# Two token tiles of the value stage in one PSUM bank, in a hybrid decoder layer

## The chip, the core and the metric

The kernel runs on one core of a Trainium2 chip. The metric is the device time of one execution in microseconds (us). A core has several engines that run beside each other, each through its own queue in order: TensorE for matmuls (PE in the profile, with its weight loads as PEld), VectorE (DVE), ScalarE (ACT), GpSimd (POOL) and SyncE (SP), which here issues nearly all DMA transfers. Matmuls write into PSUM, which the kernel uses as eight banks of 512 fp32 numbers in each of 128 partitions; ACT and DVE read the results out of it.

## The reference

One inference step of a one-layer decoder for a prompt of 1024 tokens and 64 sample tokens (8 sequences of 8), width 1024. What matters here is the first projection and its two token-major parts, the attention values v (256 columns) and the gMLP values gmlp_v (768 columns):

```python
def layer(x, norm_mix, w_in, ...):
    h = rmsnorm(x, norm_mix)
    q, k, v, gu, gv, ga, gb = split_in(h @ w_in)
    ...
    o, nk, nv = attn_prompt(q, k, v, sinks)      # or attn_sample
    vn = layernorm(jax.nn.gelu(gv), ln_g, ln_b)
    s = spatial_gating(jax.nn.gelu(gu), vn, ws, bs)
    merged = jax.nn.sigmoid(ga) * (o @ w_pa) + jax.nn.sigmoid(gb) * (s @ w_pb)
    x = x + merged @ w_out
    f, nconv = conv_ffn(rmsnorm(x, norm_ffn), w_up, conv_w, conv_b, w_down, conv_prev)
    return x + f, nk, nv, nconv, vn
```

## The kernel before

The tokens are handled in two groups: group 0 has the 64 sample tokens and the first 512 prompt tokens, group 1 the last 512. All products are made from numbers split into a high and a low part, so that one fp32 product is three matmuls (high by high, high by low, low by high).

The change lies in the **value stage**, the first stage of the kernel, from about 4.9 to 107 us of the span. There the tokens are the stationary operand and 256 columns of weights (`w2h`, `w2l`) stream past them; the result of one token tile, 128 tokens by 256 columns, takes half a PSUM bank. The sample tokens are a tile of their own ("s"): its stationary operand holds the high parts in one half of the partitions and the low parts in the other (`both` in `mm_tok`), so that it takes 16 matmuls, and its two halves are added after the read-out. A prompt tile takes 24 (8 pieces of the contraction, three matmuls each, L554).

The stage goes over its weights in eight passes of 256 columns. The first pass, gmlp_v's first third for group 0, is written out by itself with five banks at once (`ps5`), since it runs while x is still being loaded; the change leaves it alone. The other seven are calls of `tokens` (L601), in this order on PE, and are called pass 1 to 7 below:

| pass | group | columns | token tiles in order |
|---|---|---|---|
| 1 | 0 | gmlp_v, second third | s, 0, 1, 2, 3 |
| 2 | 0 | v | s, 0, 1, 2, 3 |
| 3 | 0 | gmlp_v, last third | s, 0, 1, 2, 3 |
| 4 | 1 | v | 4, 5, 6, 7 |
| 5 to 7 | 1 | gmlp_v, last, first and second third | 4, 5, 6, 7 |

For each tile `tokens` takes a bank, makes the matmuls, and calls `out`, which reads the bank: `gv_out` by one activation on ACT (gelu, with the token's scale `rst`; L596), `v_out` by one on ACT too (L569). For the sample tile both first go through `whole`: ACT copies one half out (L561), DVE adds the other half from the bank (L562), and the activation then reads the sum in SBUF. `gv_out` ends with a store by SP (`gvd`, L599). Between the tiles stand jobs for the other engines: in passes 1 and 2 `x_job`, which loads 128 rows of group 1's x into one of four buffers (`stg`, L354), splits it (`hh` on ACT, L44; `hl` on DVE, L45) and sums its squares (L667, L668).

Banks come from a pool of eight: seven that go round under the name `st` (`bank()`), and one named `mx` for the sums of squares (`stats_tok`, L499) behind which the token scales are made (`rst`: a square root on ACT, L500, and a reciprocal on DVE, L501). The tile framework makes a matmul that starts in a bank wait until the last reader of that bank is done; it tracks a bank as one whole. Between the passes `stats_all` (L511) takes banks of the same pool, and the next stage (`Chain.product`, L315) does so too.

What each engine runs, and in which order, is fixed at the end of the program by a table (`ORDER`, applied by `issue_order`): it names positions in each engine's list, so that the order stays as long as the list does.

Of the kernel before, what the change touches and what calls it, by code (L numbers as in the profile page):

```python
# [34 lines left out]
def layer(tc, a):  # L35
# [11 lines left out]
    with ExitStack() as top:  # L47
# [333 lines left out]
        with ExitStack() as ph1:  # L381
# [109 lines left out]
            def bank():  # L491
                return psa.tile([P, 512], F32, name="st")
# [53 lines left out]
            def mm_tok(ps, g, lo, w, k):  # L546
                (ah, al, both), (wh, wl) = hs[g][k], w
                if g == lo == 0:
                    todo = [(both, wh), (both, wl)]
                else:  # L550
                    ah, al = ah[:, lo:lo + P], al[:, lo - NS * (g == 0):][:, 0:P]
                    todo = [(ah, wh), (ah, wl), (al, wh)]
                for i, (u, v) in enumerate(todo):
                    PE.matmul(ps, u, v[:, k, :], start=k + i == 0, stop=k == KD - 1 and i == len(todo) - 1)  # L554
# [46 lines left out]
            def tokens(g, key, out, jobs, between=None):  # L601
                if key in (("v", 1), ("gv", 1, 2)):
                    wide[key] = wide[key[0], 0, *key[2:]]
                else:
                    W.get()
                    W.get()
                for i, (_, lo) in enumerate(groups[g]["toks"]):
                    ps = bank()[:, :256]
                    for k in range(KD):
                        mm_tok(ps, g, lo, wide[key], k)  # L610
                    if between and i == 0:
                        between()
                    out(i, ps)
                    if jobs:
                        jobs.pop(0)()
# [54 lines left out]

            jobs = [x_job(k) for k in range(KD)]
            tokens(0, ("gv", 0, 1), lambda i, ps: gv_out(0, i, 1, ps), jobs, first_out)
            tokens(0, ("v", 0), lambda i, ps: v_out(0, i, ps), jobs)
            stats_all(0)
            tokens(0, ("gv", 0, 2), lambda i, ps: gv_out(0, i, 2, ps), jobs)
            hs0o.close()
            t0h, xr = right(th0, "T0h"), right(xro, "xr")
# [352 lines left out]
            def acc2():  # L1030
                return pmm.tile([P, 1024], F32, name="mm")
# [388 lines left out]
            for c in range(KD):  # L1420
                xt = x_next(0, c)
                w, ps = W.get(), acc2()
# [60 lines left out]
            for c in range(KD):  # L1483
                xt = x_next(1, c)
                w, ps = W.get(1 if c < 7 else 4), acc2()
# [214 lines left out]
        with ExitStack() as ph3:  # L1700
# [109 lines left out]
            bank = [psd.tile([P, 512], F32, name="dn") for _ in range(6)]  # L1810
# [272 lines left out]
```

## Time and profile before

| | |
|---|---|
| time, median of 3 runs | 1491.72 us (1490.73 to 1493.11) |
| the profiled execution | 1490.81 us |
| its span, first to last instruction | 1489.1 us |
| TensorE clock granted, mean | 0.999 |
| PE busy | 99% of the span |
| DVE busy | 79% |
| ACT busy | 58% |
| POOL busy | 19% |

The span is cut by the profile into times from its first instruction, and all times below are counted so. A row of a timeline gives start, length, engine, line, operation, what it writes and reads, and how many like it were put together. A matmul's length is its latency: in a stream they begin 0.11 us apart and last 0.28 us each, so a PE that is busy all the time is not shown at its peak by that. A bracket at the end of a row tells how long the engine was idle ahead of it and who ended that.

### The profile page before, as it was taken

The numbers are of one execution on the slowest core, as the hardware profiler recorded it, in microseconds if no ns is written. First come the engines' busy times: TensorE is split into PE (matmuls) and PEld (weight loads), VectorE is DVE, ScalarE is ACT, GpSimd is POOL, SyncE is SP. The second block draws the span as 40 slices with busy tenths as digits, with TensorE's granted clock in tenths as the row PEclk, the third lists the DMA queues.
The fourth block names the chain that finished last, engine by engine and source line by source line (L and its number), as shares of the span: only waits on it lengthen the run. The fifth ranks groups of instructions, "written<-read, shape, count | busy, mean of one in ns | idle before, by whom it ended". The sixth has DMA issues, their size and how long they took to land.

```text
span 1489.1 us, 30035 instructions
## 1 busy us (share of the span) xinstructions
PE 1480.2 (99%) x11476; PEld 1445.6 (97%) x11476; DVE 1181.0 (79%) x1890; ACT 856.9 (58%) x1794; POOL 286.6 (19%) x392
## 2 busy tenths in 40 slices
PE   9999999999999999999999999999999999999998
PEld 9999999999998999998989999999999999999997
DVE  7888877655576887989578898898898888685586
ACT  8657776564465775864444554654565556363463
POOL 3002000010030222310234222332242222000002
PEclk9999999999999999999999999999999999999999
DMA  8687546764679757458977433332332316983354
GB/s 258 228 290 248 168 167 217 239 227 161 230 261 300 221 165 247 140 185 310 336 272 271 131 123 118 125 124 96 117 134 96 110 59 234 330 300 104 112 163 155
DMA packets 133791, 289.29 MB, mean 194 GB/s; under 512 B 15760, under 2 KB 35984, under 8 KB 133648
## 3 DMA queue, kind: packets, MB, share of 16 engines
q1 hardware_dynamic: 133504, 287.37, 57.6%
q8 instruction: 90, 1.47, 0.4%
q14 instruction: 53, 0.43, 0.1%
q10 hardware_dynamic: 144, 0.01, 0.0%
HBM read 198.77 MB, written 90.52 MB: 194 GB/s over the span
## 4 chain that ended last, share of the span: by engine, by line
PE 93%; DMA 2%; DVE 2%; issue 1%; ACT 1%; SPq 0%; POOL 0%; POOLq 0%; DVEq 0%; ACTq 0%
PE st L315 52%; PE mm L240 17%; PE dn L1725 11%; PE st L554 6%; PE sc L1221 2%; PE po L1272 2%; PE pt L1248 1%; DMA traw<-td 1%; DMA wraw<-wt 1%; PE mx L849 1%; DVE tl L41 1%; DVE wl L41 0%; DMA x<-xt 0%; PE po L1175 0%; ACT th L40 0%
## 5 line engine op out<-in xcount | busy, mean ns | idle before, releaser
L315 PE MATMUL st<-t,wh 128*128 128x288 f32 x2128 | 427.6, 294 | 0.0
L315 PEld LDWEIGHTS st<-t,wh 128*128 128x128 f32 x2128 | 335.6, 188 | 0.2
L315 PE MATMUL st<-t,wl 128*128 128x288 f32 x1064 | 311.8, 293 | 0.0
L315 PE MATMUL st<-th,wh 128*128 128x256 f32 x1064 | 294.6, 277 | 0.0
L315 PE MATMUL st<-tl,wh 128*128 128x256 f32 x1064 | 294.2, 277 | 0.0
L315 PE MATMUL st<-th,wl 128*128 128x256 f32 x1064 | 293.9, 276 | 0.0
L315 PEld LDWEIGHTS st<-th,wh 128*128 128x128 f32 x1064 | 199.8, 188 | 0.2 <-ACT kn L296 0.2
L315 PEld LDWEIGHTS st<-t,wl 128*128 128x128 f32 x1064 | 199.7, 188 | 0.0
L315 PEld LDWEIGHTS st<-th,wl 128*128 128x128 f32 x1064 | 199.7, 188 | 0.0
L315 PEld LDWEIGHTS st<-tl,wh 128*128 128x128 f32 x1064 | 199.7, 188 | 0.0
L40 ACT CAST wh<-wraw 128x512 fp32r<-128x512 f32 (+2 forms) x188 | 129.2, 700 | 87.4 <-DMA wraw<-wt 28.0
L1725 PE MATMUL dn<-th,wh 128*128 128x288 f32 (+1 forms) x616 | 176.8, 287 | 0.1
L1725 PE MATMUL dn<-tl,wh 128*128 128x288 f32 (+1 forms) x616 | 176.2, 286 | 0.0
L1725 PE MATMUL dn<-th,wl 128*128 128x288 f32 (+1 forms) x616 | 175.3, 285 | 0.0
L41 DVE TENSOR_TENSOR wl<-wraw,wh 128x512 fp32r<-128x512 f32 (+2 forms) x188 | 148.6, 804 | 26.4 <-ACT wh L40 24.4
L40 ACT CAST wh<-ws 128x512 fp32r<-128x512 f32 x168 | 102.7, 621 | 87.0 <-PE st L315 53.2
L41 DVE TENSOR_TENSOR wl<-ws,wh 128x512 fp32r<-128x512 f32 x168 | 117.5, 709 | 42.5 <-ACT wh L40 41.8
L1725 PEld LDWEIGHTS dn<-th,wh 128*128 128x128 f32 x616 | 115.6, 188 | 0.5 <-DVE x L1735 0.4
L1725 PEld LDWEIGHTS dn<-th,wl 128*128 128x128 f32 x616 | 115.9, 188 | 0.1
L1725 PEld LDWEIGHTS dn<-tl,wh 128*128 128x128 f32 x616 | 115.6, 188 | 0.1
L41 DVE TENSOR_TENSOR tl<-traw,th 128x544 fp32r<-128x544 f32 (+1 forms) x85 | 61.1, 723 | 21.1 <-ACT th L40 20.9
L40 ACT CAST th<-traw 128x544 fp32r<-128x544 f32 (+1 forms) x85 | 54.5, 642 | 38.2 <-PE dn L1725 29.2
(292 smaller groups left out, 3187.2 us busy)
## 6 DMA issues: line engine op xcount, KB each, us to landing
wraw<-wt SPq DMA_DIRECT2D x137, 512.0 KB
traw<-td SPq DMA_DIRECT2D x77, 272.0 KB
td<-za SPq DMA_DIRECT2D x22, 544.0 KB
q<-qd SPq DMA_DIRECT2D x16, 512.0 KB
upd<-hl SPq DMA_DIRECT2D x14, 512.0 KB
td<-t SPq DMA_DIRECT2D x11, 544.0 KB
wpart<-wt SPq DMA_DIRECT2D x22, 256.0 KB
qd<-q SPq DMA_DIRECT2D x8, 576.0 KB
```

Of the source, the lines that this page charges most:

```text
L40: S.copy(hi, src)
L41: V.tensor_sub(lo, src, hi.bitcast(F32))
L240: PE.matmul(ps[:, lo:lo + c1 - c0], u[:, k, :], v[:, c0:c1], start=(k == 0 and i == 0), stop=(k == nk - 1 and i == 2))
L315: PE.matmul(ps, u[:, kk, :], v, start=first and kk + i == 0, stop=kk == 3 and i == 2, skip_group_check=True)
L554: PE.matmul(ps, u, v[:, k, :], start=k + i == 0, stop=k == KD - 1 and i == len(todo) - 1)
L849: PE.matmul(ps[:, P * i:P * i + P], vn[:, i], late["wst"][:, c, :], start=True, stop=True)
L1221: PE.matmul(ps[:, h, o0:256], q, kst[kv][:, e, k0:cur + P], start=e == 0, stop=e == 1)
L1248: PE.transpose(pt[:, h * P:h * P + P], s[:, h, 0:P], ident)
L1272: PE.matmul(po, v[:, kv, :], t, start=e == 0, stop=last)
L1725: PE.matmul(place(m, e), u[:, m, :], v[:, lo:hi], start=new and i + k == 0 and (e == 0 or m % 2 == 0), stop=i == NU - 1 and k == 2, skip_g ...
```

## The change

In `tokens` the first tile and the third now share one bank, the second and the fourth another, each with a half of 256 columns; the fifth, where there is one, has a bank to itself. A pass of group 0 takes three banks in place of five, one of group 1 two in place of four. No instruction comes or goes, and every engine keeps its order.

```diff
@@ def tokens(g, key, out, jobs, between=None) @@
                 else:
                     W.get()
                     W.get()
+                banks = []
                 for i, (_, lo) in enumerate(groups[g]["toks"]):
-                    ps = bank()[:, :256]
+                    if i in (0, 1, 4):
+                        banks.append(bank())
+                    ps = banks[(0, 1, 0, 1, 2)[i]][:, 256 * (i in (2, 3)):][:, :256]
                     for k in range(KD):
                         mm_tok(ps, g, lo, wide[key], k)
```

What it changes is the bank that a matmul writes, and with it what the matmul waits for. PE's rows at the end of pass 1's second tile and the start of its third, before (`st` with its number is the bank's allocation, `h0` and so on the tokens, `w2h` and `w2l` the weights):

```order
L554 MATMUL st_579<-w2l_471,h7_444 128x256
L554 MATMUL st_579<-w2h_470,h7_444 128x256
L554 MATMUL st_616<-w2h_470,h0_296 128x256 [waits Activation_49]
L554 MATMUL st_616<-w2l_471,h0_296 128x256
L554 MATMUL st_616<-w2h_470,h0_296 128x256
```

And of the change, at the same place:

```order
L554 MATMUL st_579<-w2l_471,h7_444 128x256
L554 MATMUL st_579<-w2h_470,h7_444 128x256
L554 MATMUL st_517<-w2h_470,h0_296 128x256 [waits DVE_49]
L554 MATMUL st_517<-w2l_471,h0_296 128x256
L554 MATMUL st_517<-w2h_470,h0_296 128x256
```

The third tile waited for an activation of the pass before, the reader of a bank seven allocations back. Now it goes into `st_517`, the bank of the pass's own first tile, the sample's, and waits for DVE's addition out of it.

The start of pass 2's fourth tile on PE, before:

```order
L554 MATMUL st_815<-w2l_510,h7_444 128x256
L554 MATMUL st_815<-w2h_509,h7_444 128x256
L554 MATMUL st_860<-w2h_509,h0_296 128x256 [waits Activation_49]
L554 MATMUL st_860<-w2l_510,h0_296 128x256
L554 MATMUL st_860<-w2h_509,h0_296 128x256
```

And of the change:

```order
L554 MATMUL st_735<-w2l_510,h7_444 128x256
L554 MATMUL st_735<-w2h_509,h7_444 128x256
L554 MATMUL st_774<-w2h_509,h0_296 128x256 [waits Activation_49]
L554 MATMUL st_774<-w2l_510,h0_296 128x256
L554 MATMUL st_774<-w2h_509,h0_296 128x256
```

Both wait for ACT, but the one before for the activation that read pass 1's second tile, the one of the change for the activation that reads pass 2's own second tile, `st_774`.

## The prediction

> **What bounds the kernel now.** I read the page first: the busy times, then the chain that ended last.
>
> ```profile
> span 1489.1 us, 30035 instructions
> ...
> PE 1480.2 (99%) x11476; PEld 1445.6 (97%) x11476; DVE 1181.0 (79%) x1890; ACT 856.9 (58%) x1794; POOL 286.6 (19%) x392
> ...
> PE 93%; DMA 2%; DVE 2%; issue 1%; ACT 1%; SPq 0%; POOL 0%; POOLq 0%; DVEq 0%; ACTq 0%
> ```
>
> PE is the path: 93% of the chain. An average can hide stages with another limit, so the view of busy times by stretch comes next, from the end of the load-bound start (20 us) to the last matmuls; the first two numbers of a row are its length and PE's busy time.
>
> ```profile
> 20.00:107.00 87.00, 87.00 (x760) 86.56 (x759) 77.14 (x141) 57.90 (x107) 0.01 (x1) 1.00 0.78 253
> 107.00:447.00 340.00, 340.00 (x2776) 339.81 (x2775) 239.28 (x394) 206.02 (x413) 44.00 (x57) 1.00 0.64 213
> 447.00:660.00 213.00, 212.96 (x1464) 196.25 (x1463) 175.65 (x336) 145.46 (x438) 52.75 (x94) 1.00 0.63 203
> 660.00:1100.00 440.00, 440.00 (x3247) 425.03 (x3246) 372.06 (x519) 229.50 (x421) 120.34 (x152) 1.00 0.52 184
> 1100.00:1480.00 380.00, 379.88 (x3099) 379.27 (x3097) 300.15 (x474) 200.41 (x388) 53.88 (x68) 1.00 0.50 165
> ```
>
> The first row is the stretch in which all seven passes of the change run, the others are everything behind it. PE idles 0.00 us in the first and 0.04 + 0.12 us in the rest. The view of waits, from 20 us on, has one row for PE:
>
> ```profile
> PE fs L1770 <- DVE rt L1762: 0.6, 1, 0.6
> ```
>
> That row, at the very end, waits for work that itself waits for PE. Two things follow. The seven banks never hold PE up now, so taking fewer of them can win nothing. And a microsecond that PE loses before 107 us finds no gap behind it in which to be made good: it goes into the time whole, less at most 0.16 us.
>
> **What the change removes and adds.** No instruction is added, removed or moved. What goes are PE's waits for a bank seven allocations old, which cost 0.0 us by the row above. What comes: the third tile's first matmul waits until the first tile has been read out of the bank, and the fourth's until the second has. Before, a read-out could be late by several tiles; now it has one tile, the one between. So for each pass I compare the time at which PE reached the third and fourth tile with the end of the read-out that it must now wait for. PE's rows for pass 1 (start, length; in a row of x2 the second matmul starts 0.11 later, and it is the first of a tile):
>
> ```profile
> 26.30 0.39 PE L554 MATMUL st<-w2h,h 128*128 128x256 f32 x2
> 29.02 0.39 PE L554 MATMUL st<-w2h,h 128*128 128x256 f32 x2
> 31.74 0.39 PE L554 MATMUL st<-w2h,h 128*128 128x256 f32 x2
> 41.71 0.39 PE L554 MATMUL st<-w2h,h 128*128 128x256 f32 x2
> ```
>
> Third, fourth and fifth tile of pass 1 begin at 26.41, 29.13 and 31.85: 2.72 us for a tile of 24 matmuls. The last row is the fourth tile of pass 2, at 41.82. The read-outs of pass 1, from the timelines of DVE and ACT:
>
> ```profile
> 27.56 0.75 DVE L562 TENSOR_TENSOR gs<-st,gs 64x256 f32<-64x256 f32 x2
> 31.00 0.47 ACT L596 ACTIVATE gv<-st,rst 128x256 f32<-128x256 f32 x1
> ```
>
> The sample tile is read by a copy on ACT and then by the addition L562 on DVE; the second of the two in the row is pass 1's and ends at 28.31. The second tile's activation ends at 31.47. They are late because both engines first finish the pass before (whose scale, a square root, comes late) and the next group's x.
>
> Two small prices of a wait come from the first microseconds, where PE does wait:
>
> ```profile
> 7.44 0.75 DVE L538 SCALAR_TENSOR_TENSOR h<-x,c_gains,h 128x512 fp32r<-128x512 f32 x1 [0.61 <-ACT h L536]
> 8.24 0.51 PE L554 MATMUL st<-w2h,h 128*128 128x256 f32 x2 [0.17 <-DVE h L538]
> 7.34 0.39 PE L554 MATMUL st<-w2h,h 128*128 128x256 f32 x2
> ```
>
> DVE ends at 8.19 and PE starts at 8.24: 0.05 us from release to start. And the two matmuls behind that wait take 0.51 us where two in the stream take 0.39: 0.12 us for starting again.
>
> **Pass 1.** Third tile: 28.31 + 0.05 = 28.36, a stop of 1.95 us. Fourth: PE could be there at 28.36 + 0.12 + 2.72 = 31.20 but the read-out allows 31.47 + 0.05 = 31.52, 2.39 behind its old 29.13. These two stops are not added: read-outs that ACT and DVE do at their own pace set the hour. Fifth tile: 31.52 + 0.12 + 2.72 = 34.36, so PE is 2.51 us late.
>
> **Pass 2** depends on how much of this lateness ACT takes over. What stands queued behind the stop is all of PE's stream; who waits for it is ACT, with the fifth tile's read-out, then SP with its store, then two loads of x behind that store, then ACT again:
>
> ```profile
> 36.41 0.46 ACT L596 ACTIVATE gv<-st,rst 128x256 f32<-128x256 f32 x1
> 36.90 0.32 SPq L599 DMA_DIRECT2D gvd<-gv  x1
> 37.31 0.88 SPq L354 DMA_DIRECT2D stg<-xt  x2
> 42.68 0.72 ACT L44 ACTIVATE hh<-stg,c_gains 128x512 fp32r<-128x512 f32 x1 [0.99 <-DMA stg<-xt]
> 43.95 0.47 ACT L569 ACTIVATE gv<-st,rst 128x256 f32<-128x256 f32 x1
> ```
>
> The fifth tile now ends at 34.36 + 2.72 + 0.17 (a matmul's length beyond its share of the stream, 0.28 - 0.11) = 37.25, so ACT reads it at 37.30 in place of 36.41: 0.89 late. The store and both loads go out 0.89 later, the last load lands 0.89 later, and pass 2's second tile is read out at 44.42 + 0.89 = 45.31. The fourth tile starts at 45.36 against 41.82: PE is now 3.54 late, 3.66 with the restart. The two ends of this term: the loads may land when they did (a busy queue, not the issue, setting the hour), then ACT's wait of 0.99 us swallows the 0.89 and PE is 44.42 + 0.05 - 41.82 + 0.12 = 2.77 late; or ACT falls behind as far as PE, 2.77 + 2.51 = 5.28. I take 3.66, since SP issues in order and the two loads stand right behind the store.
>
> **Passes 3 to 7.** The rows of DVE, ACT and PE, in that order:
>
> ```profile
> 55.05 0.41 DVE L562 TENSOR_TENSOR gs<-st,gs 64x256 f32<-64x256 f32 x1
> 57.42 0.84 ACT L596 ACTIVATE gv<-st,rst 128x256 f32<-128x256 f32 x2
> 53.15 0.39 PE L554 MATMUL st<-w2h,h 128*128 128x256 f32 x2
> 61.63 0.47 ACT L596 ACTIVATE gv<-st,rst 128x256 f32<-128x256 f32 x1 [2.25 <-PE st L554]
> 67.48 0.48 ACT L569 ACTIVATE gv<-st,rst 128x256 f32<-128x256 f32 x1
> 67.86 0.28 PE L554 MATMUL st<-w2h,hh 128*128 128x256 f32 x1
> 79.14 0.47 ACT L596 ACTIVATE gv<-st,rst 128x256 f32<-128x256 f32 x1
> 79.87 0.28 PE L554 MATMUL st<-w2h,hh 128*128 128x256 f32 x1
> ```
>
> Pass 3: the third tile began at 53.26, now 56.92; the addition ended at 55.46, with ACT's 0.89 at 56.35: no stop. The fourth, at 55.98 + 3.66 = 59.64, has its read-out by 57.89 + 0.89. At 61.63 ACT has waited 2.25 us for PE: from here both engines shift by PE's 3.66, and only the old distances count. Pass 4: the read-out ended at 67.96, the third tile began at 67.86, so 68.01 - 67.86 = 0.15 of stop, and 0.12. Pass 5: read out at 79.61, 0.26 before the tile's 79.87; passes 6 and 7 come with more to spare. No stop there.
>
> **The sum** is 3.66 + 0.15 + 0.12 = 3.9 us. The profiled execution took 1490.81 us (span 1489.1), so it would be 1494.7; the median of the three runs shown, 1491.72, lies 0.91 above that execution, and the forecast stands on the median: **1495.6 us**.
>
> **Rivals.** *Nothing is lost: a later PE wait makes the time good, or the new wait does not bind* (not slower, 1491.7). Its place is behind 107 us, and it needs a PE wait of 3.9 us on something that does not wait for PE, such as a weight load. The stretches above show 0.16. For the second half: a wait is listed by engine, but its count in the built program is that of the second L562 addition for pass 1's third tile. Chance 0.09.
>
> *The x loads land when they did*: 2.77 + 0.27 = 3.0 us, 1494.8 on the median. For it: ACT's row at 42.68 waits for a load, and the DMA share is 0.78. Against: both loads stand behind the store on SP. Chance 0.12.
>
> *ACT falls behind as far as PE in pass 2*: 5.28 + 0.27 = 5.6 us, 1497.3. Against it: ACT reached the fifth tile at 36.41, 1.7 us after PE had done with it (31.85 + 2.72 + 0.17). Chance 0.06.
>
> *The clock drops in a stop.* At the start PE ran slower:
>
> ```profile
> 1.10:4.40 3.30, 3.25 (x15) 3.25 (x16) 0.81 (x3) 2.04 (x3) 0.76 (x2) 1.00 0.72 193
> 4.59 0.39 PE L620 MATMUL st<-c_ones 128*128 128x128 f32 x2
> ```
>
> 15 matmuls in 3.30 us are 0.22 each, and a little later the same pair is 0.11 apart (0.39 - 0.28). If a stop put PE back into that pace for another 3.3 us, half of it, 1.6 us, is lost: 1497.3. Against it: the short waits between 5 and 10 us did not slow PE, and the stop is one of 1.95 us. Chance 0.06. [...]
>
> **How the numbers follow.** Forecast 0.64, the four rivals 0.09, 0.12, 0.06 and 0.06, and 0.03 for a gain that I see no cause for. The range goes from the lowest run shown plus the low end (1490.73 + 3.04 = 1493.8, taken down to 1493.4 as the runs shown differ by 2.4 us) to 1497.6, which takes in the two dear rivals; nothing lost lies outside. A measurement of this kernel can tell about 0.2%, 2.98 us, from no change. The forecast passes that by 0.9 us, so of its 0.64 some 0.08 counts as the same; of the low rival two thirds. Slower 0.56 + 0.04 + 0.12 = 0.72, same 0.08 + 0.08 + 0.09 = 0.25, faster 0.03.
>
> **What would show it.** PE waits for DVE L562 once, about 1.95 us near 26.4; for ACT L596, about 0.3 near 31; for ACT L569, about 1.0 near 44 (PE there at 41.82 + 2.51 = 44.33, released at 45.36), and 0.15 near 71; no others. The busy row of the first stretch would lose PE busy time by these stops, 3.45 us, less the 0.17 us tail of the matmul before each, some 2.8 us, and every later stage would keep its old length. A stop of PE in passes 3, 5, 6 or 7, or a later stage of another length, would prove me wrong.

## The result, and the profile after

| | before | with the change |
|---|---|---|
| median | 1491.61 us (16 runs, 1490.42 to 1494.23) | 1495.60 us (16 runs, 1494.11 to 1496.67) |
| ratio | 1 | 1.0024, 95% interval 1.0016 to 1.0031 |
| profiled execution, span | 1490.81 us, 1489.1 us | 1494.11 us, 1492.4 us |

The kernel is 4.0 us slower by the medians. The profiled execution of the change was the fastest of its 16 runs; it is 3.30 us above the profiled one of before, and the account below is of these 3.30 us. One of the 12 runs of the longer stop below took 1831.76 us at a mean granted clock of 0.75, and the ratio given there is without it.

The busy times, the chain that ended last, and the stretches, in the same views and columns as for before:

```profile
PE 1482.6 (99%) x11476; PEld 1448.2 (97%) x11476; DVE 1181.3 (79%) x1890; ACT 858.2 (58%) x1794; POOL 286.3 (19%) x392
...
PE 97%; ACT 1%; DMA 1%; issue 0%; SPq 0%; DVE 0%; POOL 0%; POOLq 0%; ACTq 0%
```

```profile
20.00:107.00 87.00, 85.07 (x727) 84.09 (x728) 74.83 (x137) 57.69 (x105) 0.00 (x0) 1.00 0.75 243
107.00:447.00 340.00, 340.00 (x2774) 339.80 (x2774) 239.00 (x396) 203.85 (x409) 43.52 (x56) 1.00 0.64 212
...
1100.00:1480.00 380.00, 380.00 (x3099) 379.62 (x3098) 300.66 (x473) 202.40 (x388) 52.48 (x68) 1.00 0.50 164
```

The first stretch now has 1.93 us in which PE is idle, where it had none. The view of PE's waits says for what:

```profile
PE st L554 <- DVE gs L562: 1.7, 1, 1.7
...
PE fs L1773 <- DVE rt L1765: 0.6, 1, 0.6
PE st L554 <- ACT gv L596: 0.2, 1, 0.2
```

One wait for the addition L562, one short one for L596, and none for L569. In the timelines of DVE and PE (start, length) these are the third and fourth tile of pass 1; then come the fourth tile of pass 2 and the third of pass 4:

```profile
27.36 0.75 DVE L562 TENSOR_TENSOR gs<-st,gs 64x256 f32<-64x256 f32 x2
```

```profile
28.16 0.39 PE L554 MATMUL st<-w2h,h 128*128 128x256 f32 x1 [1.72 <-DVE gs L562]
28.39 0.28 PE L554 MATMUL st<-w2l,h 128*128 128x256 f32 x1
...
31.32 0.38 PE L554 MATMUL st<-w2h,h 128*128 128x256 f32 x1 [0.15 <-ACT gv L596]
...
44.03 0.39 PE L554 MATMUL st<-w2h,h 128*128 128x256 f32 x2
44.26 0.28 PE L554 MATMUL st<-w2l,h 128*128 128x256 f32 x1
...
70.07 0.28 PE L554 MATMUL st<-w2h,hl 128*128 128x256 f32 x1
70.32 0.39 PE L554 MATMUL st<-w2h,hh 128*128 128x256 f32 x1
70.55 0.28 PE L554 MATMUL st<-w2l,hh 128*128 128x256 f32 x1
```

The addition ends at 28.11 and PE starts 0.05 us later; the next matmul follows after 0.23 in place of 0.11, the price of starting again. The fourth tile of pass 2 begins in the stream at 44.15 (the second matmul of the row at 44.03): no stop there. Pass 4's third tile begins 0.25 after the matmul before it, a stop of about 0.13.

That is some 2.8 us of stops and restarts. The rest is no wait: the matmuls of passes 5 to 7 follow each other more slowly. Their stretch, from the first tile's start to the time at which the next matmul would follow the last one, before and after (length first, PE's instructions in the second brackets):

```profile
74.33:107.07 32.74, 32.74 (x291) 32.74 (x290) 31.77 (x56) 18.71 (x34) 0.00 (x0) 1.00 0.93 298
```

```profile
76.70:110.71 34.01, 34.01 (x292) 34.01 (x290) 31.67 (x56) 18.84 (x34) 0.00 (x0) 1.00 0.91 298
```

The same 288 matmuls of L554 at the same granted clock of 1.00 take 1.27 us more: 4.4 ns each, 117.7 ns from start to start in place of 113.3.

How far PE is behind is best read by taking the same matmul in both traces and the difference of its start:

| matmul | before | after | PE late by |
|---|---|---|---|
| pass 1, first | 20.41 | 20.20 | -0.21 |
| pass 1, third tile | 26.41 | 28.16 | 1.75 |
| pass 1, fifth tile | 31.85 | 34.17 | 2.32 |
| pass 2, fourth tile | 41.83 | 44.15 | 2.32 |
| pass 4, first | 61.43 | 63.74 | 2.31 |
| pass 4, third tile | 67.86 | 70.32 | 2.46 |
| pass 5, first | 74.33 | 76.70 | 2.37 |
| pass 7, last tile | 104.35 | 107.88 | 3.53 |
| at 1300 us | | | 3.82 |
| at 1330 us | | | 3.32 |

Pass 1 adds 2.5 us, pass 2 and 3 nothing, pass 4 some 0.15 by its first stop, and passes 5 to 7 the 1.27 us; between 1300 and 1330 us half a microsecond is made good. There PE had a stop of its own before:

```profile
1313.55 0.29 PE L1725 MATMUL dn<-th,wl 128*128 128x288 f32 x1
1313.96 0.40 PE L1725 MATMUL dn<-th,wh 128*128 128x288 f32 x1
1314.20 0.29 PE L1725 MATMUL dn<-tl,wh 128*128 128x288 f32 x1
```

0.41 between two starts where 0.13 is usual, and 0.24 to the next: 0.39 us; the other 0.11 is a slower pace for a few dozen matmuls behind it. PE waits there until DVE has read the bank (L1735, L1738 in the change). In the change PE comes 3.82 us later, and DVE starts to read 3.02 us later (1315.45 for 1312.43), so PE no longer stops. That is how this execution fell out; in others below DVE is later still, and the stop is longer.

### The profile page after: what moved, and what is told of

Its sections match the earlier page's. It is cut to its first block, busy times and chain, and to the rows that moved or that the text cites. A ratio compares the mean times of both kernels' runs of the same rounds, so it can differ in the third digit from the quotient of the medians.

```text
span 1492.4 us, 30035 instructions
## 1 busy us (share of the span) xinstructions
PE 1482.6 (99%) x11476; PEld 1448.2 (97%) x11476; DVE 1181.3 (79%) x1890; ACT 858.2 (58%) x1794; POOL 286.3 (19%) x392
## 4 chain that ended last, share of the span: by engine, by line
PE 97%; ACT 1%; DMA 1%; issue 0%; SPq 0%; DVE 0%; POOL 0%; POOLq 0%; ACTq 0%
PE st L315 52%; PE mm L240 17%; PE dn L1728 15%; PE st L554 5%; PE sc L1224 2%; PE po L1275 2%; PE pt L1251 1%; DMA wraw<-wt 1%; PE mx L852 1%; PE po L1178 0%; ACT h L536 0%; ACT gv L596 0%; POOL x L1804 0%; PE st L511 0%; PE po L1174 0%
## 5 line engine op out<-in xcount | busy, mean ns | idle before, releaser
L1728 PE MATMUL dn<-th,wh 128*128 128x288 f32 (+1 forms) x616 | 176.6, 287 | 0.0
L1728 PE MATMUL dn<-tl,wh 128*128 128x288 f32 (+1 forms) x616 | 176.2, 286 | 0.0
L1728 PE MATMUL dn<-th,wl 128*128 128x288 f32 (+1 forms) x616 | 175.3, 285 | 0.0
L41 DVE TENSOR_TENSOR wl<-ws,wh 128x512 fp32r<-128x512 f32 x168 | 117.7, 711 | 43.9 <-ACT wh L40 43.2
L1728 PEld LDWEIGHTS dn<-th,wl 128*128 128x128 f32 x616 | 115.9, 188 | 0.1
L1728 PEld LDWEIGHTS dn<-tl,wh 128*128 128x128 f32 x616 | 115.7, 188 | 0.1
L1728 PEld LDWEIGHTS dn<-th,wh 128*128 128x128 f32 x616 | 115.6, 188 | 0.1
```

What stands on the lines that cost most here:

```text
L41: V.tensor_sub(lo, src, hi.bitcast(F32))
L1728: PE.matmul(place(m, e), u[:, m, :], v[:, lo:hi], start=new and i + k == 0 and (e == 0 or m % 2 == 0), stop=i == NU - 1 and k == 2, skip_g ...
```

## The experiments

All but the last of them replace the fixed places by one line that says, for each pass, which bank a tile takes; `key` is the pass (`("gv", 0, 1)` is pass 1, `("v", 1)` is pass 4), `(0, 1, 2, 3, 4)` is a bank for each tile as before:

```diff
                 banks = []
+                place = (0, 1, 0, 1, 2) if ... else (0, 1, 2, 3, 4)
                 for i, (_, lo) in enumerate(groups[g]["toks"]):
-                    if i in (0, 1, 4):
+                    second = place[i] < len(banks)
+                    if not second:
                         banks.append(bank())
-                    ps = banks[(0, 1, 0, 1, 2)[i]][:, 256 * (i in (2, 3)):][:, :256]
+                    ps = banks[place[i]][:, 256 * second:][:, :256]
```

Below only this line is shown. Lines behind `tokens` stand 2 further down than in the change, and 5 further down than in before (L1725 of before is L1728 in the change and L1730 here). "PE late" is against the profiled execution of before, as in the table above.

### Pass 1 alone

```diff
+                place = (0, 1, 0, 1, 2) if key == ("gv", 0, 1) else (0, 1, 2, 3, 4)
```

> Only pass 1 shares banks (first tile with third, second with fourth); passes 2 to 7 keep a bank for each tile. Theory (a tile waits for the read-out of the tile two places ahead, and each stop is the old lateness of that read-out): PE stops about 1.95 us for DVE L562 and 0.3 us for ACT L596, is 2.5 us late at the fifth tile of pass 1, and stops nowhere else: 2.5 us over before, about 1494.1. Rival (the whole loss is one price for each shared pair, 13 or 14 pairs in all): a seventh of 3.9, some 0.6 us.

Measured: 1495.28 us (9 runs) against 1491.27 (30 runs of before), ratio 1.0025 [1.0015, 1.0034]. That is 4.0 us, as much as the whole change and 1.5 more than pass 1 was to cost. Its PE rows, at pass 1's third tile and at 454 us:

```profile
28.85 0.38 PE L554 MATMUL st<-w2h,h 128*128 128x256 f32 x1 [1.80 <-DVE gs L562]
...
453.68 0.28 PE L315 MATMUL st<-th,wl 128*128 128x256 f32 x1
454.84 1.09 PE L1131 MATMUL sc<-cache,qs 128*64 128x128 f32 x16 [0.88 <-issue]
```

The stop in pass 1 is the forecast one, and its 2.5 us are there. Two things came on top. First the clock. Two neighbouring stretches of this trace (length, PE busy, ..., granted clock as third number from the end):

```profile
26.66:30.08 3.42, 1.62 (x14) 1.42 (x13) 2.89 (x8) 3.40 (x9) 0.00 (x0) 1.00 0.87 264
30.08:33.49 3.41, 3.41 (x18) 3.41 (x17) 3.11 (x6) 2.51 (x6) 0.00 (x0) 0.50 0.73 222
```

From 30.08, 1.2 us behind the end of the stop, PE ran at half the clock for 3.41 us: PE is 3.72 later at the end of pass 1 than at its start, 1.22 more than the stops make.

Second, a wait 420 us later. The profile names nobody for the 0.88 us at 454.84 ("issue"). DVE's timeline shows what ends just before:

```profile
454.33 0.41 DVE L301 TENSOR_TENSOR z<-k,st 128x256 f32<-128x256 f32 x1
```

The addition ends at 454.74, 0.10 ahead of PE's start, and reads a bank of the same pool. In before the score matmul did not wait: it starts at 449.70, ahead of the same addition (450.14). Pass 1 alone takes two banks fewer from a rotation of seven, so every later tile lands two banks further back; the full change takes 14 fewer, two whole turns, and later tiles keep their banks. Lateness is not the cause: the kernel of the longer stop below, which takes one bank fewer, is 4.43 us late at this place and has no wait. That PE waits for this addition is read from the times alone; that the shift of two banks puts it there is worked out, and no run took the shift alone.

### All passes but pass 1

```diff
+                place = (0, 1, 0, 1, 2) if key != ("gv", 0, 1) else (0, 1, 2, 3, 4)
```

> Passes 2 to 7 share, pass 1 keeps five banks. Theory: the stops are set by the hour of the read-outs, not by their number, so pass 2 now pays by itself: third tile 40.12 + 0.05 - 39.11 = 1.06 us, fourth tile late by 44.42 + 0.05 - 41.82 = 2.65 in all, with a restart 2.77; pass 4 0.27; together 3.0 us, about 1494.6, and with e1 5.5, more than the whole change. Rival (the stops add up): 3.9 - 2.5 = 1.4 us, 1493.0.

Measured: 1494.46 us (10 runs), ratio 1.0023 [1.0013, 1.0032], 3.2 us over before. So the parts cost 4.0 and 3.2 alone and 4.0 together. The 4.0 of pass 1 alone can hold the clock and the late wait too; by the stops in the traces, passes 1 and 2 cost 2.5 and some 1.5 alone, and 2.5 and nothing together. The stops do not add. PE's rows at pass 2's third tile:

```profile
40.36 0.39 PE L554 MATMUL st<-w2h,h 128*128 128x256 f32 x1 [0.77 <-DVE gs L562]
40.59 0.28 PE L554 MATMUL st<-w2l,h 128*128 128x256 f32 x1
```

Here PE arrives on time and meets a stop that it never sees when pass 1 has made it late: it is 0.33 late before and 1.39 after, 1.06 more. The fourth tile adds only some 0.4, restart included, where 1.4 was due by the read-out's old hour, and again the slow pace of 118 ns runs through passes 5 to 7 (1.27 us), here from pass 2's fourth tile on through pass 3 too. The total is near the forecast, its parts are not. The reason for the fourth tile is on ACT:

```profile
39.80 0.72 ACT L44 ACTIVATE hh<-stg,c_gains 128x512 fp32r<-128x512 f32 x1
...
40.89 1.56 ACT L44 ACTIVATE hh<-stg,c_gains 128x512 fp32r<-128x512 f32 x2
43.00 0.47 ACT L569 ACTIVATE gv<-st,rst 128x256 f32<-128x256 f32 x1
```

The last `hh` starts at 41.73 (40.89 + 1.56 - 0.72) and waits for no load; in the prediction's trace it started at 42.68 after a wait of 0.99.

### Passes 5 to 7 alone, and a pairing with more room

```diff
+                place = (0, 1, 0, 1, 2) if key[0] == "gv" and g == 1 else (0, 1, 2, 3, 4)
```

> Only passes 5 to 7 share. Theory: every read-out there ends 0.2 us or more before its tile begins, no stop, the time of before (within 0.5 us), and matmuls of these passes 113 ns apart as before. Rival (sharing itself slows the stream: in the trace of the change the matmuls of passes 5 to 7 are 118 ns apart, of before 113): 288 matmuls by 4.4 ns, 1.3 us over before, and 118 ns in this trace.

```diff
+                place = (0, 1, 2, 0, 1) if True else (0, 1, 2, 3, 4)
```

> All seven passes take as few banks as the change (three or two), but first tile shares with fourth and second with fifth, so that a read-out has two tiles of time, 5.4 us, in place of one. Theory: read-outs end before their time (pass 1 28.31 for 29.13 and 31.47 for 31.85; pass 2 40.12 for 41.82 and 44.42 for 44.54), no stop, within 0.5 us of before. Rival (fewer banks, or two tiles in one bank, cost by themselves): like the change, 3.9 us over before.

Measured: 1491.41 us (11 runs), ratio 1.0003 [0.9994, 1.0012], for the first; 1491.38 us (11 runs), ratio 0.9997 [0.9988, 1.0006], for the second, in which all passes share, the first tile with the fourth and the second with the fifth (a pass of group 1 so takes three banks, not the two that the expectation names). Neither has a wait of PE at a shared bank. Writing one half of a bank after the other half has been read cost nothing in itself that these two runs show (ratios 1.0003 and 0.9997), and with two tiles between, in place of one, every read-out is in time. What cost time in the runs above is a read-out that ends after the next writer has arrived (1.80 us of stop in pass 1 alone), and one tile more between the two is enough to avoid it here.

The second kernel's profiled execution was its slowest (1495.66 us). Its PE rows far behind the value stage show why:

```profile
1315.53 0.38 PE L1730 MATMUL dn<-th,wh 128*128 128x288 f32 x1 [1.78 <-DVE x L1740]
...
1316.46 0.61 PE L1730 MATMUL dn<-th,wh 128*128 128x288 f32 x1 [0.29 <-DVE x L1740]
```

It is the place at which before stops for 0.39 us; here it stops longer, with 3.41 us at half clock behind it. PE is 0.30 us late ahead of it and 4.15 at 1330 us. So an execution can lose some four microseconds at a place that the change does not touch.

### The change again, twice

The same program as the change, with the places written as above.

> The change once more, for a second execution under the profile. Theory A (what the forecast says of pass 2): the fourth tile of pass 2 stops when ACT's wait for the last load of x lasts as before, so here about 1 us. Theory B: passes 5 to 7 at 118 ns a matmul cost 1.2 us in every execution. Theory C: a stop that lies within one window of 3.4 us halves the clock for the next 3.4 us (seen in e1 at 30 us), here in about half of the executions, for some 1.2 us.

> A third execution of the change under the profile, on the same three questions: a stop in pass 2 (A, about 1 us), 118 ns in passes 5 to 7 (B, every time if the pace follows from the program), half clock after the stop of pass 1 (C, in about half of the executions).

Measured, one run each with no interval: 1495.95 and 1496.87 us, against 1491.13 (21 runs of before). In both, pass 1 costs 2.5 and 2.6 us, the fourth tile of pass 2 has no stop, and passes 5 to 7 go at 118 ns. What differs: the first starts pass 1 already 1.1 us late, and has a stop in pass 3 that was not foreseen:

```profile
56.80 0.28 PE L554 MATMUL st<-w2h,h 128*128 128x256 f32 x1
57.38 0.38 PE L554 MATMUL st<-w2h,h 128*128 128x256 f32 x1 [0.30 <-DVE gs L562]
```

The second has the pace of 118 ns from pass 1's fourth tile through pass 3 as well, 1.1 us, and loses 0.7 us more behind 1330 us. Neither drops the clock.

### Pass 4 alone, and all passes but pass 4

These ask whether the stop in pass 4 sets the slow pace behind it.

```diff
+                place = (0, 1, 0, 2) if key == ("v", 1) else (0, 1, 2, 3, 4)
```

> Only pass 4's first and third tile share, the smallest part of the change that stops PE at all (0.15 us for ACT L569 and 0.12 for the restart). Theory B (a short stop in pass 4 leaves the matmuls behind the next change of instruction in the slower pace): 118 ns in passes 5 to 7, which is 288 matmuls by 4.4 ns or 1.27 us, less 0.2 for pass 4's own faster end: 1.3 us over before. Rival (the pace has nothing to do with the stop): 113 ns there, 0.3 us over before.

```diff
+                place = (0, 1, 0, 1, 2) if key != ("v", 1) else (0, 1, 2, 3, 4)
```

> The change without pass 4's sharing. Theory B: pass 4 as before, passes 5 to 7 back at 113 ns, 1.3 us under the change, some 2.5 to 3.5 over before. Rival: 118 ns there as in the change, and only the stop of 0.27 gone.

Measured: 1493.21 us (11 runs), ratio 1.0010 [1.0001, 1.0019], for pass 4 alone; 1494.86 us (11 runs), ratio 1.0022 [1.0013, 1.0031], without pass 4. The first is 2.1 us by the medians, and its interval takes in both answers, 0.3 and 1.3 us, so the time does not tell them apart. The traces refute the simple form: pass 4 alone had 118 ns in passes 5 to 7, but in passes 1 to 3 too, where its program is that of before; and the kernel without pass 4's sharing had 118 ns in passes 2, 3 and 5 to 7.

### A longer stop: second tile with fourth, in pass 1

```diff
+                place = (0, 1, 2, 1, 3) if key == ("gv", 0, 1) else (0, 1, 2, 3, 4)
```

> Only pass 1 shares, and only one pair: the second tile with the fourth; all else as before. Theory (the read-out's hour sets the loss, stops do not add): one stop of 31.47 + 0.05 - 29.13 = 2.39 us for ACT L596 and 0.12 for the restart, PE 2.5 us late at the fifth tile, as much as with both pairs. Rival (each pair pays its own stop): 0.3 us, the second stop of the forecast. Theory C on the clock (half for 3.4 us when a window of 3.4 us has 1.97 us or more without a matmul, as in e1; not with 1.88 in e6 or 1.95 in e8): this longer stop halves it whenever it lies within one window, in about a third to a half of the executions, so 2.5 to 4 us over before, and by the clock records of the trace.

> The same kernel as e9 for a second execution under the profile, for theory C: half clock behind the stop if 1.97 us or more of it lie within one window (windows follow the clock records by multiples of 3.413 us), full clock if the window's edge cuts it.

Only the fourth tile now waits, for ACT's late read-out of the second. Measured: 1494.30 us (12 runs) against 1491.70 (17 runs), ratio 1.0015 [1.0006, 1.0024]; the same program a second time, one run, 1496.16. The first trace's row at the stop, and two stretches, ahead of the drop of the clock and in it:

```profile
31.81 0.39 PE L554 MATMUL st<-w2h,h 128*128 128x256 f32 x1 [2.25 <-ACT gv L596]
```

```profile
29.59:33.00 3.41, 1.19 (x10) 1.19 (x11) 3.12 (x7) 3.38 (x8) 0.00 (x0) 1.00 0.71 219
33.00:36.41 3.41, 3.41 (x19) 3.41 (x18) 1.59 (x4) 0.82 (x3) 0.00 (x0) 0.50 0.57 146
```

PE lost 2.5 us by the stop and 1.64 more by the clock, 2.5 and 1.57 in the second trace. Behind the stop, with 2.2 us of it inside one such stretch, the granted clock was 0.50 for 3.41 us both times.

### Before again

> The kernel before, for a second execution under the profile. If the pass 2 term of the forecast was sized by one late load: ACT's last split of x (L44) starts 0.5 to 1 us earlier here than the 42.68 us of the trace before, as in e2, e3 and e7 (41.7, 41.6, 42.1). If 42.68 is the rule for this kernel, again 42.6. PE's stop near 1313 us, 0.28 us in the trace before and about 2 in e4, is somewhere between, and the matmuls of passes 5 to 7 are 113 ns apart as in before, e1, e3 and e4, or 118 if the pace is the execution's luck.

Measured, one run: 1492.70 us. The last `hh` of pass 2 started at 42.58, near the 42.68 of the first trace, so a late load was no accident of that one execution. It is no rule either: with passes 5 to 7 alone and with pass 4 alone, the program is that of before up to there, and it started at 41.62 and 42.05. And this unchanged program has the slow pace in passes 5 to 7 (the stretch ends at the last matmul's start, 0.11 us sooner than the two rows for these passes in the section on the result):

```profile
75.50:109.40 33.90, 33.90 (x291) 33.90 (x290) 31.98 (x56) 18.84 (x34) 0.00 (x0) 1.00 0.87 285
```

## Why the prediction was right, and where it was not

The time was forecast at 1495.6 us and the median is 1495.60. Its first term held in all its parts; one term was wrong by its whole size, and something outside the sum took its place.

**Pass 1: right.** The third tile was to stop for 1.95 us and stopped for 1.89 (28.16 against 26.27, when the stream would have had it). The fourth was to stop 0.32 more; PE was due at 28.16 + 0.12 + 2.72 = 31.00 and started at 31.32. Forecast 2.51 us late, measured 2.5 in the change and 2.5 and 2.6 in its repeats. That the two stops do not add, because the read-outs set the hour, is what the second experiment shows from another side. The prices of 0.05 and 0.12 us held.

**Pass 2: the step that failed** is "I take 3.66, since SP issues in order and the two loads stand right behind the store". The first links held: the fifth tile was read late, and store and loads went out later. SP's and ACT's rows of the change (L670 is the L667 of before):

```profile
37.59 0.32 SPq L599 DMA_DIRECT2D gvd<-gv  x1
38.01 0.86 SPq L354 DMA_DIRECT2D stg<-xt  x2
```

```profile
37.09 0.47 ACT L596 ACTIVATE gv<-st,rst 128x256 f32<-128x256 f32 x1 [0.63 <-PE st L554]
...
41.30 1.32 ACT L44 ACTIVATE hh<-stg,c_gains 128x512 fp32r<-128x512 f32 x2
42.65 0.63 ACT L670 ACTIVATE stg<-stg 128x512 f32<-128x512 f32 x1
43.30 0.48 ACT L569 ACTIVATE gv<-st,rst 128x256 f32<-128x256 f32 x1
```

The loads were issued 0.70 us later (38.01 against 37.31). But the last `hh` starts at 41.90, 0.78 *earlier* than in before, and without a wait: the last load had landed no later than 3.5 us after its issue, where it had taken 4.9. The read-out of the second tile ended at 43.78, PE came at 44.15, and the stop was 0, not 1.15 us with its restart. The same held in both repeats and in the kernel without pass 4's sharing: all four traces in which passes 1 and 2 both share as in the change have it so. The nearest rival, that the loads land when they did, was right that the issue need not set the hour, but its price was too high: the last load was there sooner than in before, and nothing was lost. In the six executions without a stop in pass 1 the last `hh` started between 41.6 and 42.7 although the loads went out within 0.4 us of each other, so a single trace's landing time was no fixed point to add 0.89 to. Why the loads came quicker was not tried and stays open.

**Passes 3 to 7: the stops right, but for one.** Pass 4 stopped for 0.13 and paid 0.12 (forecast 0.15 and 0.12); passes 3 and 5 to 7 had no stop in the profiled execution, and passes 5 to 7 cost nothing when they alone share. One repeat had a stop of 0.5 in pass 3, which the prediction had denied and named as a sign against itself.

**What the sum left out: the pace.** That "every later stage would keep its old length" was wrong for passes 5 to 7 by 1.27 us, another sign that the prediction named against itself. With pass 2's 1.15 us gone, this is why the total fits; the agreement of the profiled execution is in part luck. It is no cost of the shared bank as such, since passes 5 to 7 sharing alone kept 113 ns, and the unchanged program had 118 ns once.

**That a lost microsecond "finds no gap behind it": wrong by half a microsecond.** The 0.12 us of PE's idle time in the last stretch counted only the time without any matmul in flight. By starts, the same stop was 0.28 long and its restart 0.11, with 0.11 of slower pace behind it. The change saves all 0.50, and so do six other traces, one of them of the unchanged program; but three traces in which PE also came later (by 0.3 to 4.0 us) stopped there longer than before.

**The clock.** The rival was given 1.6 us behind a stop of 1.95. It did not happen in the three traces of the change, and did in pass 1 alone (1.22 us) and in both traces of the longer stop (1.6 us). Its price was near, and its cause was seen there: a granted clock of 0.50 for 3.41 us behind the stop. In the traces of the change no stretch of 3.413 us, laid out as in the last section, held more than 1.88 us of the stop. In pass 1 alone the half clock followed the stretch 26.66 to 30.08 above, in which PE was busy for 1.62 of 3.42 us.

**Still open.** What sets the pace of 113 or 118 ns, and so how the 4.0 us of the median divide: the three traces of the change give 2.5 to 2.6 us for pass 1 and 1.27 for passes 5 to 7, with other terms from run to run, but a trace shows one execution, and before's own runs, too, differ in pace and at 1313 us.

## What to carry to other kernels

Tiles that share a bank need the slowest read-out between them: compare, tile by tile, when the next writer arrives with when the last reader ends, and pair the tiles that lie furthest apart, since here one tile more between the two left nothing of the 4.0 us. Stops of an engine that waits for others' hours need not add: here passes 1 and 2 cost 2.5 and some 1.5 us alone and 2.5 together, since with one stop taken away another appeared where PE now came early. A term that rests on when a transfer landed in a single trace needs a range from landing early to landing late, and a total that fits is only evidence after its terms have been looked at one by one.

## What the runs showed of the hardware

**Half clock behind a stop of some 2 us.** The clock records of before and of the change hold one stretch at 1.00 each, from 4.43 to 1485.81 and from 7.36 to 1485.33 us: 1481.38 and 1477.97 us, 434 and 433 times 3.4133. The four drops behind a stop lasted 3.41 us each. On that ground each trace is laid out here in stretches of 3.413 us from where its clock changes; the expectations call such a stretch a window. The halved stretches followed ones in which PE, by starts of its matmuls, stood still for 1.97 us (pass 1 alone), 2.2 (both longer stops) and 2.3 (the kernel with more room, at 1313 us); behind ones with 1.88 (a repeat) and 1.95 us (without pass 4) the clock stayed at 1.00. The nearest case that stayed, the stretch of the latter and the one behind it:

```profile
24.90:28.32 3.42, 1.63 (x15) 1.43 (x13) 2.88 (x7) 3.38 (x9) 0.00 (x0) 1.00 0.84 262
28.32:31.73 3.41, 3.23 (x25) 3.03 (x26) 2.90 (x6) 3.38 (x8) 0.00 (x0) 1.00 0.74 220
```

By busy time the two are 0.01 us apart, 1.63 here and 1.62 in the one that was followed by half clock. By standing still they are 0.02 us apart, 1.95 and 1.97. That rests on one trace on each side, and no run varied the length of a stop by itself, so what in a stretch decides is not shown. In the change's own profiled execution the stop of 1.89 us was cut in two by the edge of a stretch at 27.84: PE was busy for 2.03 us of the stretch ahead of it and for 3.01 of the one behind it, both at 1.00.

**Two paces of the same matmul.** Products of 128 by 256 with a new weight each (L554) followed every 113 or 118 ns, at a granted clock of 1.00. In before they went at 113.3 up to the sums of squares in pass 4 (L499, 64.15 us), at 117.8 behind these, and at 113.3 again behind the sums between passes 4 and 5 (L511, until 74.33). In the change they went at 113.3 from the end of pass 1's stops, at 117.8 behind L499 (66.47), at 113.4 behind the stop in pass 4 (70.07 to 70.32), and at 117.8 behind L511 (until 76.70). In all five traces with a stop in pass 4, the change, its two repeats, all passes but pass 1 and pass 4 alone, passes 5 to 7 were slow, after fast and slow passes alike; without one they were fast in before, pass 1 alone, passes 5 to 7 alone and the kernel with more room, and slow without pass 4 and in before again. That the stop in pass 4 turns the passes behind it slow is read from the change's trace and is not proved.

**A place far behind the change moves the time.** The place near 1313 us stops PE in the traces of before, of pass 4 alone, of the second trace of the longer stop and of the kernel with more room, for 0.3 to 2.1 us. In the last, with 3.4 us of half clock behind it, the execution took 1495.66 us where its median was 1491.38. There DVE's read-out came 2.50 us later than in before (1314.93 for 1312.43), and ACT, in the work queued ahead of it, had waited for a load:

```profile
1309.18 0.65 ACT L40 CAST th<-traw 128x544 fp32r<-128x544 f32 x1 [2.05 <-DMA traw<-td]
```

In before the same cast, at 1306.46, had waited 0.69. The program alone does not decide it: of the two traces of before, and of the two of the longer stop, one each has the stop and one has none. What made DVE late in the others was not followed, and how much of the spread of the runs comes from this place is not shown.
